# A hybrid attention decoder step on one core: the second sum of exponentials moves to PSUM and takes every second key tile, ScalarE casts the filler weights, and the masks of the row maxima go in pairs

## The chip, the cores and the metric

One core of a Trainium2 chip. The metric is the device time of one execution in microseconds (us), the median of several executions. PE is TensorE, PEld its weight loads, DVE is VectorE, ACT is ScalarE, POOL is GpSimd, SP the engine whose queue issues most DMAs.

## What is computed

One decoder layer: 2,048 prompt positions of width 1,024, and eight single decode positions with 512 cached positions each. The part that the change touches is the prompt's attention, eight heads of 64:

```python
s = einsum('bqhd,bkhd->bhqk', qb, kf) * SCALE
s = s + cb[:, :, :, None] - c[:, :, None, :]        # cumulated log forget gates
s = where(pos_k <= pos_q, s, -inf)
pr = softmax(s, axis=-1)
return einsum('bhqk,bkhd->bqhd', pr, vf)
```

Around it stand an input projection of 3,592 columns (q, k, v, forget gate, and the gates and operands of a chunked spatial mixing), silu gates, and an output projection of 1,024 by 1,024.

## The kernel before

The kernel has three stages. The first, up to about 590 us, makes the input projection in split precision: each fp32 operand is a rounded part (`hi`, the fp32r type) plus a remainder (`lo`), and three matmuls stand for one product. The second, 590 to 1181 us, is the prompt's attention with leftover projection work woven in. The third, from 1181 us, is the output projection.

**Attention, per head.** Two passes run over the scores. `maxima` (L897) takes each of the 16 query tiles (128 rows) in turn: it multiplies the tile with all keys at or before it, in pieces of at most 512 keys (`pieces`), each piece into one PSUM bank of the tag `tp`; on a tile's last piece a second small matmul adds the causal mask (weights `identb`, data `maskb`, both bf16, L917). A DVE minimum over the piece (L918, `mn`) frees the bank; signs are flipped, so a minimum is the row maximum. After four query tiles `shifts` (L926) turns the maxima and stores them as a row of the augmented queries.

`values` (L963) then takes one unit, 512 queries `c` of a head `h`, over its 4c+4 key tiles `kt`: two score matmuls into a bank of tag `sc` (with a mask on the diagonal tiles), one exponential on ACT into a ring tile `p` (L982), and, every eight tiles, a batch of `av` matmuls (`run_av`) that add `p` times the values into a bank of tag `av` (L1004). When a unit ends, ACT copies the upper half of `av` out (L1009, `at`) and DVE adds the lower half (L1010).

**The softmax denominators.** Beside that, the `p` tiles are summed for the denominators. POOL keeps the sum `acc` in SBUF (L989, L995) and takes most tiles. DVE keeps a second sum `accd` in SBUF: tiles 2 and 3 together (L991), then tiles 7 and 11 (L993), of units with c > 0. Two tiles into the diagonal (kt = 4c+1) POOL adds `accd` to `acc` (L997). Some 5 us of PE work later PE turns `acc` and DVE sums it (`add_up`, L1013 to L1019).

**Fillers.** Between these steps `fill` deals out matmuls of the projection that are left (tag `fl`) and, later, of the output projection. Their weights come 128 columns at a time (`fill_weights`, L772): POOL scales the raw rows by the norm's gain (L779, four instructions), POOL rounds them to `hi` (L781), POOL subtracts for `lo` (L782). The output projection's weights are rounded by ACT (`split`, L243) and subtracted by DVE (L248).

**Order.** PE's instructions run in the order in which the code emits them; the yields of `maxima`, `values` and the fillers interleave them, and `later` places follow-up work a set amount of PE work further on. The other engines run their own instructions in an order that a planner fixed beforehand by modelled times, each engine strictly one after another: an instruction that waits holds all behind it on its engine.

**PSUM.** The eight banks of stage 2 are dealt out in L1258: `sc` 2, `tp` 3 (also for all transposes), `av` 2, `fl` 1. In stage 3 the two halves of each output tile use `sc` and `av` (L1157). The 12 pieces of maxima that come before 590 us use a `tp` of two banks.

Of the kernel before, what the change touches and what calls it, by code (L numbers as in the profile page):

```python
# [9 lines left out]
F32 = mybir.dt.float32  # L10
# [4 lines left out]
ALU = mybir.AluOpType  # L15
AX = mybir.AxisListType
# [3 lines left out]
P = 128  # L20
# [5 lines left out]
HD = 64  # L26
# [23 lines left out]
FGAP = 1500.0  # L50
NSC = 2
NTP = 3
NAV = 2
UNITS = [(h, c) for h in range(6) for c in range(4)] + [(6, 0), (6, 1), (6, 2), (7, 0), (6, 3), (7, 1), (7, 2), (7, 3)]
AHEAD = 0.8
QLEAD = 6
# [22 lines left out]
def hymba_step(ctx, tc, x_prompt, x_sample, cache_k, cache_v, cache_logf, page_table, g_norm, w_in,  # L79
# [3 lines left out]
    nc = tc.nc  # L83
# [28 lines left out]
    def tname(t):  # L112
        cnt[0] += 1
        return f"{t}_{cnt[0]}"
# [10 lines left out]
    def s2(dt=F32, t="s2"):  # L125
        return wk.tile([P, 512], dt, tag="t2", name=tname(t))
# [6 lines left out]
    def bank(tag, n=512):  # L133
        pool, bufs = pool_of[tag]
        return pool.tile([P, n], F32, tag=tag, bufs=bufs, name=tname(tag))
# [37 lines left out]
    def mm(out, lhsT, rhs, start, stop, ns):  # L173
        Pe.last = nc.tensor.matmul(out, lhsT, rhs, start=start, stop=stop).ins  # L174
        pe(ns)
# [596 lines left out]
    def fill_weights(o, pair=None):  # L772
        hi, lo = (t.rearrange("p (k f) -> p k f", k=KT) for t in pair or (s4(F32R, "fh"), s4(F32R, "fl")))
        got = []

        def halves(half, raw):
            for k in range(4):
                kk = 4 * half + k
                nc.gpsimd.tensor_scalar(raw[:, k], raw[:, k], gT[:, kk:kk + 1], 0.0, op0=ALU.mult, op1=ALU.add)  # L779
            sl = slice(4 * half, 4 * half + 4)  # L780
            nc.gpsimd.tensor_scalar(hi[:, sl], raw, 1.0, 0.0, op0=ALU.mult, op1=ALU.add)  # L781
            nc.gpsimd.tensor_tensor(lo[:, sl], raw, hi[:, sl].bitcast(F32), op=ALU.subtract)  # L782
            got.extend((hi[:, k], lo[:, k]) for k in range(4 * half, 4 * half + 4))
        for half in range(2):
            raw = raw2().rearrange("p (k f) -> p k f", k=4)
            nc.sync.dma_start(raw, w[half * 512:(half + 1) * 512, o:o + P].rearrange("(k p) f -> p k f", p=P))
            later(FLAG * (1 + half), lambda half=half, raw=raw: halves(half, raw))
        return got
# [78 lines left out]
    def pieces(nk):  # L867

        n = (nk + 511) // 512
        if nk % n == 0 and (nk // n) % 2 == 0 and nk // n >= 256:  # L870
            return [(a * (nk // n), nk // n) for a in range(n)]
        return [(a * 512, min(512, nk - a * 512)) for a in range(n)]
# [24 lines left out]
    def maxima(hd):  # L897

        h = hd["h"]
        nxt = qhi.pop() if qhi else load_hi(h, 0)  # L900
        for c in range(2):
            q = nxt
            for i in range(8 * c, 8 * c + 8):
                if i == 2:
                    nxt = load_hi(h, 1)
                if i == 10 and h + 1 < NH:
                    qhi.append(load_hi(h + 1, 0))
                cut = pieces((i + 1) * P)
                if i % 4 == 0:
                    part = sm.tile([P, 4, len(cut)], F32, tag="mn", bufs=3, name=tname("mn"))  # L910
                for n, (c0, m) in enumerate(cut):
                    sp = bank("tp")[:, :m]
                    end = n == len(cut) - 1
                    mm(sp, q[:HD + 2, (i % 8) * P:(i % 8 + 1) * P], hd["k2"][:HD + 2, c0:c0 + m], True, not end,
                       max(m, 256) * 0.422)
                    if end:
                        mm(sp[:, m - P:], identb, maskb[:, 0], False, True, 56)  # L917
                    nc.vector.tensor_reduce(part[:, i % 4, n:n + 1], sp, axis=AX.X, op=ALU.min)  # L918
                    yield m * 0.422
                if i % 4 == 3:  # L920
                    shifts(h, i // 4, part)

    shifted = set()
# [39 lines left out]
    def values(at):  # L963
# [3 lines left out]
        for kt in range(4 * c + 4):  # L967
# [12 lines left out]
            p = ring[nt[0] % len(ring)]  # L980
            nt[0] += 1
            nc.scalar.activation(p[:, n0:], sp[:, n0:], AF.Exp, bias=zero1, scale=-1.0)  # L982
            if kt == 0 or kt == 2 and c:
                p0 = p
            elif kt == 1:
                if n0:
                    nc.gpsimd.memset(p[:, :n0], 0.0)
                    n0 = 0
                nc.gpsimd.tensor_tensor(acc, p0, p, op=ALU.add)  # L989
            elif kt == 3 and c:  # L990
                nc.vector.tensor_tensor(accd, p0, p, op=ALU.add)  # L991
            elif kt % 4 == 3 and kt < 4 * c:
                nc.vector.tensor_tensor(accd, accd, p, op=ALU.add)  # L993
            else:
                nc.gpsimd.tensor_tensor(acc[:, n0:], acc[:, n0:], p[:, n0:], op=ALU.add)  # L995
                if kt == 4 * c + 1:
                    nc.gpsimd.tensor_tensor(acc, acc, accd, op=ALU.add)  # L997

            def step(kt=kt, p=p, n0=n0, acc=acc, c=c, st=st, at=at):

# [110 lines left out]
    def out_products(i, hi, lo, xy, tags):  # L1111
        for f in range(2):
            fs = slice(f * 512, (f + 1) * 512)
            po = bank(tags[f])
            for n, k in enumerate(KORDER):
                wh, wl = wo_hl[k, f]
                mm(po, hi[:, k], wh, n == 0, False, 216)
                mm(po, hi[:, k], wl, False, False, 216)
                mm(po, lo[:, k], wh, False, n == KT - 1, 216)
                yield 648  # L1120
            nc.vector.tensor_tensor(xy[:, fs], xy[:, fs], po, op=ALU.add)
            yield 0
            if i == NT - 1:
                nc.scalar.dma_start(y[i * P:(i + 1) * P, fs], xy[:, fs])
        if i < NT - 1:
            nc.scalar.dma_start(y[i * P:(i + 1) * P], xy)
# [10 lines left out]
    def out_tiles():  # L1137

        gs = None
        for i in range(NT):  # L1140
            while i not in ins or not ins[i] or len(wo_hl) < 2 * KT:
                prepare(i)
                if last_phase[0]:
                    give()
                else:
                    yield -1
            for n in range(1, OAHEAD + 1):
                prepare(i + n)
            if i == 8:
                for _ in Pe.steps:  # L1150
                    pass
                while decoded[0] < B:
                    give()
                gs = decode_out()
            if gs is not None and i < 12:
                next(gs, None)
            yield from out_products(i, **ins.pop(i), tags=("sc", "av") if last_phase[0] else ("fl", "fl"))  # L1157

    mgen = all_maxima()
    mdone = [0.0]  # L1160
# [94 lines left out]

    seen = len(nc.cur_bb.bb.instructions)
    psb = ctx.enter_context(tc.tile_pool(name="psb", bufs=1, space=PSUM, reuse_waits="tile"))
    pool_of.update(sc=(psb, NSC), tp=(psb, NTP), av=(psb, NAV), fl=(psb, 1))  # L1258
    ring = []
    for t in [s8(t="p"), s8(t="p"), s4(t="p")]:  # L1260
        ring += [t[:, a:a + 512] for a in range(0, t.shape[1], 512)]
    accs = [s2(t="acc") for _ in range(2)]
    accd = s2(t="accd")
    Pe.side = 1e12
    while mdone[0] < AHEAD * MT:
        c = next(mgen)
# [66 lines left out]
```

## Time and profile before

| | |
|---|---|
| time, median of 3 runs | 1345.16 us (1342.2 to 1346.73) |
| profiled execution: its own time | 1347.51 us |
| profiled execution: span from first to last instruction | 1345.8 us |
| mean granted TensorE clock | 0.987 of 2.4 GHz |
| busy share of the span: PE, PEld, DVE, ACT, POOL | 97%, 75%, 53%, 32%, 43% |

A profile row of a group of instructions gives the line, the engine, the operation, output and input tiles with shapes, the count, then the busy time in us and the mean duration in ns, then the engine's idle time ahead of these instructions and what ended it. "issue" as the end of a wait means that the engine waited for nothing that the profile shows. Matmuls overlap, so the distance of their starts is the better measure of what one costs.

### The profile page before, as it was taken

The numbers are of one execution on the slowest core, as the hardware profiler recorded it, in microseconds if no ns is written. First come the engines' busy times: TensorE is split into PE (matmuls) and PEld (weight loads), VectorE is DVE, ScalarE is ACT, GpSimd is POOL, SyncE is SP. The second block draws the span as 40 slices with busy tenths as digits, with TensorE's granted clock in tenths as the row PEclk, the third lists the DMA queues.
The fourth block names the chain that finished last, engine by engine and source line by source line (L and its number), as shares of the span: only waits on it lengthen the run. The fifth ranks groups of instructions, "written<-read, shape, count | busy, mean of one in ns | idle before, by whom it ended". The sixth has DMA issues, their size and how long they took to land.

```text
span 1345.8 us, 19516 instructions
## 1 busy us (share of the span) xinstructions
PE 1304.6 (97%) x6544; PEld 1006.6 (75%) x6544; DVE 706.9 (53%) x1328; ACT 433.1 (32%) x781; POOL 574.6 (43%) x679
## 2 busy tenths in 40 slices
PE   6999999999999999999999999999999998999998
PEld 5999999999887877866666566666656664688877
DVE  4346654534678544266586555566565774322321
ACT  5542332222222111114453344434444456310100
POOL 3113343423223554416776666676757466400000
PEclk9999999999999999999998899999999998999999
DMA  6644353555113665634254854666375645463221
GB/s 217 188 119 112 87 142 116 155 140 158 52 48 99 187 184 148 159 97 127 78 138 85 181 138 126 177 182 169 95 192 135 172 119 196 135 238 117 107 77 49
DMA packets 170805, 183.09 MB, mean 136 GB/s; under 512 B 39402, under 2 KB 125866, under 8 KB 169138
## 3 DMA queue, kind: packets, MB, share of 16 engines
q1 hardware_dynamic: 166818, 173.08, 46.7%
q10 hardware_dynamic: 3488, 8.39, 1.6%
q8 instruction: 52, 0.85, 0.3%
q14 instruction: 47, 0.39, 0.1%
q0 software_dynamic: 400, 0.38, 0.1%
HBM read 121.53 MB, written 60.28 MB: 135 GB/s over the span
## 4 chain that ended last, share of the span: by engine, by line
PE 85%; DMA 6%; DVE 4%; ACT 2%; issue 1%; SPq 1%; POOL 1%; ACTq 0%; DVEq 0%; POOLq 0%
PE acc L174 36%; PE sc L174 15%; PE av L174 14%; PE fl L174 10%; PE tp L174 5%; PE tp L178 3%; PE pm L174 1%; DVE mn L918 1%; ACT p L982 1%; DMA xp<-in_x_prompt_dram 1%; DMA raw<-in_w_in_dram 1%; DMA q<-qk_hi 1%; DMA k<-qk_lo 1%; DMA q<-qk_lo 1%; DMA mrow<-mt 0%
## 5 line engine op out<-in xcount | busy, mean ns | idle before, releaser
L982 ACT ACTIVATE p<-sc,zero 128x512 f32<-128x512 f32 (+1 forms) x320 | 196.6, 623 | 173.9 <-PE sc L174 167.9
L995 POOL TENSOR_TENSOR acc<-acc,p 128x512 f32<-128x512 f32 (+3 forms) x184 | 194.1, 1055 | 125.2 <-ACT p L982 104.1
L918 DVE TENSOR_REDUCE mn<-tp 128x1 f32<-128x384 f32 (+6 forms) x320 | 186.9, 604 | 107.9 <-PE tp L174 105.6
L174 PE MATMUL acc<-wh,hh 128*128 128x384 f32 (+2 forms) x640 | 228.7, 357 | 0.0
L174 PE MATMUL acc<-wl,hh 128*128 128x384 f32 (+2 forms) x640 | 222.8, 348 | 1.0 <-DVE wl L256 0.9
L174 PE MATMUL acc<-wh,hl 128*128 128x384 f32 (+2 forms) x640 | 222.6, 348 | 0.6 <-DVE hl L248 0.6
L174 PE MATMUL sc<-q,k 128*128 128x512 f32 (+7 forms) x640 | 211.1, 407 | 10.6 <-ACT p L982 5.9
L174 PEld LDWEIGHTS sc<-q,k 128*128 128x128 f32 (+1 forms) x640 | 118.2, 197 | 35.3 <-ACT p L982 16.3
L174 PE MATMUL av<-p,vst 128*64 128x512 f32 (+3 forms) x640 | 135.4, 543 | 0.0
L174 PEld LDWEIGHTS acc<-wh,hh 128*128 128x128 f32 x640 | 120.7, 189 | 7.2 <-ACT hh L243 0.2
L174 PEld LDWEIGHTS acc<-wl,hh 128*128 128x128 f32 x640 | 120.9, 189 | 6.3 <-DVE wl L256 2.0
L174 PEld LDWEIGHTS acc<-wh,hl 128*128 128x128 f32 x640 | 120.3, 188 | 6.3 <-DVE hl L248 1.2
L174 PE MATMUL tp<-k,q 66*128 66x384 f32 (+6 forms) x320 | 120.3, 392 | 3.9 <-DVE mn L918 3.3
L236 POOL TENSOR_SCALAR sm<-sm 128x6 f32<-128x6 f32 (+3 forms) x84 | 20.3, 241 | 238.8 <-DVE sm L389 170.4
L174 PEld LDWEIGHTS av<-p,vst 128*64 128x64 f32 x640 | 47.9, 137 | 67.1 <-issue 57.6
L237 POOL TENSOR_TENSOR sm<-sm,mhalf 128x6 f32<-128x6 f32 (+3 forms) x84 | 89.6, 1067 | 6.7
L174 PE MATMUL sc<-wo,am 128*128 128x512 f32 x360 | 84.5, 390 | 0.0
L174 PE MATMUL av<-wo,am 128*128 128x512 f32 x360 | 84.2, 389 | 0.0
L174 PEld LDWEIGHTS tp<-k,q 66*128 66x128 f32 x320 | 61.2, 193 | 26.6 <-DVE mn L918 6.6
L174 PE MATMUL acc<-hh,wh 128*128 128x512 f32 x192 | 76.3, 397 | 4.9 <-DVE s L378 4.9
L174 PEld LDWEIGHTS av<-wo,am 128*128 128x128 f32 x360 | 67.5, 188 | 14.2
L174 PEld LDWEIGHTS sc<-wo,am 128*128 128x128 f32 x360 | 67.4, 188 | 14.1
(218 smaller groups left out, 2087.2 us busy)
## 6 DMA issues: line engine op xcount, KB each, us to landing
raw<-in_w_in_dram SPq DMA_DIRECT2D x40, 256.0 KB
kb<-in_cache_k_dram SPq DMA_DIRECT2D x32, 256.0 KB
k<-qk_hi SPq DMA_DIRECT2D x16, 512.0 KB
q<-qk_hi SPq DMA_DIRECT2D x64, 128.0 KB
vb<-in_cache_v_dram SPq DMA_DIRECT2D x32, 256.0 KB
g<-gm SPq DMA_DIRECT2D x16, 512.0 KB
xy<-in_x_prompt_dram SPq DMA_DIRECT2D x16, 512.0 KB
out_dram<-xy ACTq DMA_DIRECT2D x15, 512.0 KB
```

Source lines behind the costliest of these rows:

```text
L174: Pe.last = nc.tensor.matmul(out, lhsT, rhs, start=start, stop=stop).ins
L178: Pe.last = nc.tensor.transpose(out, in_, idn).ins
L236: nc.gpsimd.tensor_scalar(r, ss, inv_n, EPS, op0=ALU.mult, op1=ALU.add)
L237: nc.gpsimd.tensor_tensor(r, r, mhalf[:rows, :n], op=ALU.pow)
L918: nc.vector.tensor_reduce(part[:, i % 4, n:n + 1], sp, axis=AX.X, op=ALU.min)
L982: nc.scalar.activation(p[:, n0:], sp[:, n0:], AF.Exp, bias=zero1, scale=-1.0)
L995: nc.gpsimd.tensor_tensor(acc[:, n0:], acc[:, n0:], p[:, n0:], op=ALU.add)
```

## The change

- **Accumulator.** `accd` becomes a PSUM bank of a new tag `ad`; `av` goes from two banks to one. In units with c > 0, DVE copies tile 2 into `accd` and adds tiles 3, 5, 7, ... below 4c. POOL takes tiles 0 and 1, the even ones from 4 on, and the diagonal. The final sum of both moves from POOL to DVE. The SBUF buffer of `accd` goes back to the work pool. In stage 3 the second half of each output tile uses `ad`.
- **Filler weights.** The rounding to `hi` (L781) moves from POOL to ACT.
- **Maxima.** Query tiles go in pairs. The first tile's last piece is left open, its mask and minimum pending; the second tile begins with its own last piece; then come both masks, both minima, and the second tile's other pieces. `shifts` is called after the second pair of four tiles, as before after the fourth tile.

```diff
-NAV = 2
+NAV = 1
...
-            nc.gpsimd.tensor_scalar(hi[:, sl], raw, 1.0, 0.0, op0=ALU.mult, op1=ALU.add)
+            nc.scalar.copy(hi[:, sl], raw)
...
+                cuts = [pieces((j + 1) * P) for j in (i, i + 1)]
+                ends = []
+                for j, cut in zip((i, i + 1), (cuts[0], cuts[1][::-1])):
+                    for (c0, m) in cut:
+                        n = cuts[j - i].index((c0, m))
+                        end = n == len(cut) - 1
+                        sp = bank("tp")[:, :m]
+                        mm(sp, q[...], hd["k2"][:HD + 2, c0:c0 + m], True, not end, max(m, 256) * 0.422)
+                        if end:
+                            ends.append((sp, m, j, n))
+                            if j > i:
+                                for (sp, m_, _, _) in ends:
+                                    mm(sp[:, m_ - P:], identb, maskb[:, 0], False, True, 56)
+                                for (sp, _, j_, n_) in ends:
+                                    nc.vector.tensor_reduce(part[:, j_ % 4, n_:n_ + 1], sp, axis=AX.X, op=ALU.min)
+                        else:
+                            nc.vector.tensor_reduce(part[:, j % 4, n:n + 1], sp, axis=AX.X, op=ALU.min)
+                        yield m * 0.422
...
-            if kt == 0 or kt == 2 and c:
+            if kt == 0:
                 p0 = p
...
-            elif kt == 3 and c:
-                nc.vector.tensor_tensor(accd, p0, p, op=ALU.add)
-            elif kt % 4 == 3 and kt < 4 * c:
+            elif kt == 2 and c:
+                accd = bank("ad")
+                nc.vector.tensor_copy(accd, p)
+            elif kt % 2 == 1 and kt < 4 * c:
                 nc.vector.tensor_tensor(accd, accd, p, op=ALU.add)
             else:
                 nc.gpsimd.tensor_tensor(acc[:, n0:], acc[:, n0:], p[:, n0:], op=ALU.add)
                 if kt == 4 * c + 1:
-                    nc.gpsimd.tensor_tensor(acc, acc, accd, op=ALU.add)
+                    nc.vector.tensor_tensor(acc, acc, accd, op=ALU.add)
...
-            yield from out_products(i, **ins.pop(i), tags=("sc", "av") if last_phase[0] else ("fl", "fl"))
+            yield from out_products(i, **ins.pop(i), tags=("sc", "ad") if last_phase[0] else ("fl", "fl"))
...
-    pool_of.update(sc=(psb, NSC), tp=(psb, NTP), av=(psb, NAV), fl=(psb, 1))
+    pool_of.update(sc=(psb, NSC), tp=(psb, NTP), av=(psb, NAV), fl=(psb, 1), ad=(psb, 1))
...
-    accd = s2(t="accd")
```

## Rows read from the trace of the kernel before

**Rows 1.** The page: busy time of each engine, its share of the span and its instructions; and the granted TensorE clock in 40 slices of the span, in tenths.
```profile
PE 1304.6 (97%) x6544; PEld 1006.6 (75%) x6544; DVE 706.9 (53%) x1328; ACT 433.1 (32%) x781; POOL 574.6 (43%) x679
...
PEclk9999999999999999999998899999999998999999
```

**Rows 2.** Busy time by stretch: the stretch and its length, then busy us and instructions of PE, PEld, DVE, ACT and POOL, the granted clock, the DMA share and GB/s.
```profile
590.00:1100.00 510.00, 497.88 (x2458) 319.99 (x2459) 318.67 (x573) 221.74 (x402) 327.96 (x367) 0.98 0.55 141
1100.00:1181.00 81.00, 75.03 (x316) 45.14 (x315) 37.20 (x48) 38.29 (x66) 45.53 (x38) 0.92 0.53 167
1181.00:1345.80 164.80, 161.11 (x715) 130.38 (x713) 41.79 (x51) 12.82 (x14) 1.29 (x1) 1.00 0.33 118
```

**Rows 3.** The waits of PE between 590 and 1181 us: who waited for whom, us in total, times, the longest.
```profile
PE sc L174 <- ACT p L982: 5.9, 10, 1.5
PE sc L174 <- DMA q<-qk_hi: 3.9, 3, 2.5
PE tp L174 <- DVE mn L918: 3.3, 4, 2.3
PE fl L174 <- DVE sz L490: 1.3, 1, 1.3
```

**Rows 4.** Groups of instructions by form, the whole span: the masks of the maxima, and the weight loads of all masks (those of the maxima and those of the scores).
```profile
L174 PE MATMUL tp<-maskb,identb 128*128 128x128 bf16 x128 | 29.9, 233 | 0.0
...
L174 PEld LDWEIGHTS <-identb 128*128 128x128 bf16 x256 | 25.0, 98 | 39.2 <-issue 30.7
```

**Rows 5.** Timeline of PE about one masked piece (start us, duration us, what).
```profile
925.02 0.39 PE L174 MATMUL tp<-k,q 66*128 66x512 f32 x1
925.25 0.23 PE L174 MATMUL tp<-maskb,identb 128*128 128x128 bf16 x1
925.29 0.47 PE L174 MATMUL fl<-hh,fh 128*128 128x512 f32 x1
925.60 0.40 PE L174 MATMUL fl<-hl,fh 128*128 128x512 f32 x1
```

**Rows 6.** The chain of work that ended last, in order of time: one output half tile of stage 3 (start us, us, what).
```profile
1186.97 5.44 PE av L174 x24
```

**Rows 7.** Timeline of the weight loads about the masked piece of rows 5: the load for the mask.
```profile
925.24 0.10 PEld L174 LDWEIGHTS <-identb 128*128 128x128 bf16 x1 [0.27 <-issue]
```

**Rows 8.** The tile `accd`: its instructions with duration in ns (min/median/max), first and last start, form.
```profile
L991 DVE TENSOR_TENSOR accd<-p x24: 661/691/2058, 615.0 to 1144.0; 128x512 f32<-128x512 f32 x24
...
L993 DVE TENSOR_TENSOR accd<-accd,p x24: 675/1176/1737, 635.0 to 1159.8; 128x512 f32<-128x512 f32 x24
```

**Rows 9.** Groups of DVE by form between 590 and 1181 us: the two sums of `accd` in SBUF, the sum of `at` (SBUF) with `av` (PSUM).
```profile
L993 DVE TENSOR_TENSOR accd<-accd,p 128x512 f32<-128x512 f32 x24 | 27.6, 1148 | 11.8 <-ACT p L982 11.6
...
L1010 DVE TENSOR_TENSOR at<-at,av 64x512 f32<-64x512 f32 x32 | 21.6, 676 | 58.5 <-ACT at L1009 52.0 <-DMA vb<-in_cache_v_dram 3.6 <-DMA raw<-in_w_out_dram 3.0
...
L991 DVE TENSOR_TENSOR accd<-p 128x512 f32<-128x512 f32 x24 | 18.8, 785 | 8.0 <-ACT p L982 7.8
```

**Rows 10.** The tile `mxu`, where DVE multiplies one SBUF operand with one PSUM operand into SBUF (columns as in rows 8).
```profile
L507 DVE SCALAR_TENSOR_TENSOR mxu<-mxu,fl x8: 670/687/689, 642.0 to 1073.6; 128x512 f32<-128x512 f32 x8
```

**Rows 11.** Groups of POOL by form between 590 and 1181 us: sums of whole tiles, the final sum, the rounding of filler weights.
```profile
L995 POOL TENSOR_TENSOR acc<-acc,p 128x512 f32<-128x512 f32 x96 | 127.7, 1330 | 115.6 <-ACT p L982 101.3 <-ACT rt L1025 6.5 <-ACT mt L940 3.4
...
L997 POOL TENSOR_TENSOR acc<-acc,accd 128x512 f32<-128x512 f32 x24 | 31.7, 1320 | 1.4
...
L781 POOL TENSOR_SCALAR fh<-raw 128x512 fp32r<-128x512 f32 x22 | 14.1, 639 | 0.5
```

**Rows 12.** Timeline of ACT about the end of a unit with c = 3: four exponentials of the diagonal tiles in one row.
```profile
891.88 2.70 ACT L982 ACTIVATE p<-sc,zero 128x512 f32<-128x512 f32 x4 [0.82 <-PE sc L174]
```

**Rows 13.** Timeline of POOL in the same place: the sum of the second of these tiles (384 columns), and the final sum.
```profile
897.74 1.00 POOL L995 TENSOR_TENSOR acc<-acc,p 128x384 f32<-128x384 f32 x1
...
899.93 1.29 POOL L997 TENSOR_TENSOR acc<-acc,accd 128x512 f32<-128x512 f32 x1
```

**Rows 14.** Timeline of DVE: an instruction that waits for ACT with others queued behind it.
```profile
720.31 2.62 DVE L684 TENSOR_TENSOR_SCAN cc<-one,lfT 64x512 f32<-64x512 f32 x1 [1.70 <-ACT lfT L683]
```

**Rows 15.** Timeline of PE behind it.
```profile
723.57 0.50 PE L174 MATMUL tp<-k,q 66*128 66x512 f32 x1 [2.33 <-DVE mn L918]
```

**Rows 16.** Busy time by stretch, the stretches before and after that wait (columns as in rows 2).
```profile
717.00:724.20 7.20, 4.87 (x29) 3.70 (x27) 4.76 (x7) 3.23 (x5) 4.86 (x6) 1.00 0.19 53
724.20:731.02 6.82, 6.82 (x18) 4.66 (x17) 5.89 (x13) 3.08 (x7) 5.38 (x7) 0.50 0.26 80
```

**Rows 17.** Groups of ACT by form between 590 and 1181 us: roundings of output weights.
```profile
L243 ACT CAST wo<-raw 128x512 fp32r<-128x512 f32 x16 | 9.3, 616 | 4.5 <-DMA raw<-in_w_out_dram 4.5
```

**Rows 18.** Timeline of ACT: such a rounding that waited for its weights.
```profile
1075.10 0.62 ACT L243 CAST wo<-raw 128x512 fp32r<-128x512 f32 x1 [3.30 <-DMA raw<-in_w_out_dram]
```

**Rows 19.** Timeline of PE behind it.
```profile
1076.36 0.39 PE L174 MATMUL sc<-q,k 128*128 128x256 f32 x1 [1.52 <-ACT p L982]
```

**Rows 20.** Timeline of DVE at the border of two units: the last read of a unit's `av`.
```profile
751.69 0.67 DVE L1010 TENSOR_TENSOR at<-at,av 64x512 f32<-64x512 f32 x1
```

**Rows 21.** Timeline of PE at the same border: the first `av` matmul of the next unit.
```profile
753.17 1.08 PE L174 MATMUL av<-p,vst 128*64 128x512 f32 x4
```

More of the change, by code (lines that the diff above doesn't have):

```diff
@@ L902, in maxima @@
             q = nxt
-            for i in range(8 * c, 8 * c + 8):
+            for i in range(8 * c, 8 * c + 8, 2):
                 if i == 2:
@@ L907, in maxima @@
                     qhi.append(load_hi(h + 1, 0))
-                cut = pieces((i + 1) * P)
                 if i % 4 == 0:
[L910 to L920, printed above, removed]
+                    part = sm.tile([P, 4, i // 4 + 1], F32, tag="mn", bufs=3, name=tname("mn"))
+                cuts = [pieces((j + 1) * P) for j in (i, i + 1)]
[5 more added lines that the diff above has]
+                        sp = bank("tp")[:, :m]
+                        mm(sp, q[:HD + 2, (j % 8) * P:(j % 8 + 1) * P], hd["k2"][:HD + 2, c0:c0 + m], True, not end,
+                           max(m, 256) * 0.422)
+                        if end:
[8 more added lines that the diff above has]
+                        yield m * 0.422
+                if i % 4 == 2:
                     shifts(h, i // 4, part)
```

## The prediction

> **What bounds the kernel now.** I read the page first, then busy time by stretch, then PE's waits, then single places. The page gives PE 97% of the span and no other engine more than 53% [rows 1]; the reader is to see that only what changes PE's own stream or makes PE wait can move the time. By stretch, the change lies almost wholly in 590 to 1181 us: there DVE is busy 318.7 + 37.2 = 355.9 of 591 us (60%), POOL 373.5 (63%), ACT 260.0 (44%), PE 572.9 (97%), while after 1181 us PE is busy throughout and the clock is full; the granted clock is 0.98 and 0.92 in the two stretches of attention, so some microseconds ran at the lower of TensorE's two levels (1.2 of 2.4 GHz) [rows 2]. PE's waits there are short: 5.9 us for ACT's exponentials, 3.9 for a load of queries, 3.3 for the minima, 1.3 for a gate on DVE [rows 3]. So what can be won is: what PE spends on masks, about 10 us of waits, and the clock lost behind them.
>
> **Masks in pairs.** There are 128 masks in the maxima, and the 256 weight loads of all masks are preceded by 39.2 us of idle weight loading [rows 4]. One place shows the price of a single: from the piece to the second matmul after it PE takes 925.60 - 925.02 = 0.58 us. Two such matmuls of 512 columns alone would take 2 x 0.227 us, by the 5.44 us that 24 of them take in stage 3 [rows 5, 6]; the mask adds 0.13 us. Of that, 0.04 us is the mask's own distance to the next start, the rest comes after it (0.31 us for a matmul that otherwise takes 0.23): the next weights load beside a mask that is too short to cover it. Pairs make 64 groups of two. Nothing in the trace has two masks in a row. The second costs between 0.04 us (its stream alone) and 0.13 (as the first), so a pair saves 0 to 0.09 us, and all of them 0 to 5.8 us. I take 0.05 for the second, near the lower end, because no other weights of a different type have to be put back between the two: 64 x 0.08 = 5.1 us, all of it on PE's path.
>
> The row of the mask's weight load shows that it starts at 925.24, when the piece before has run out, and that nothing held it [rows 7]. The Trainium skill ("TensorE: Matmul & The Clock Gate", Step-by-step: what each phase is for) says that TensorE pulls a weight load ahead of the matmul in flight, which would leave nothing to save at the mask. The trace disagrees at this place. By that rule this term would be 0.
>
> **The sum in PSUM.** Removed from DVE: 24 x 785 ns + 24 x 1148 ns = 46.4 us. These sums are uneven, 661 to 2058 ns [rows 8, 9]. DVE's sum of `at` with a PSUM operand takes 676 ns, and the product of `mxu`, full 128 partitions with one operand in PSUM, 670 to 689 [rows 9, 10]. Per head the new units c = 1, 2, 3 have 1 + 3 + 5 sums, 3 copies and 3 final sums, so 72, 24 and 24 in all; at 0.68 us each (no row has DVE writing PSUM; 0.5 to 0.75 for the copies and sums is my bound) that is 81.6 us. DVE goes up by 35 us, from 60% to 66%. POOL loses 24 whole-tile sums, 24 final sums and 22 roundings: 31.9 + 31.7 + 14.1 = 77.7 us, from 63% to 50% [rows 11]. None of this is on PE's path by itself. PE pays only where DVE comes late: 3.3 + 1.3 us of waits now, and the clock behind them. More work on DVE speaks for more of that, the end of the 1.1 to 2 us sums, behind which minima queue, for less. Bounds: all of the 4.6 us gone, or as much again; I take -1.5 us, as the long instructions weigh more than the mean load at 66%. A `tp` bank is now held for one step more and two minima come at once, which eats one of about three steps of slack; I leave that in the bounds.
>
> **The final sum on DVE.** It must wait for POOL's sum of tile 4c+1, and all of DVE's queue waits with it: minima behind it, then PE's next `tp` bank; POOL in turn waits for DVE before the next diagonal tile. At one border the four diagonal exponentials end by 894.58, but POOL reaches the second of them at 897.74 and ends it at 898.74, more than 4 us late [rows 12, 13]. POOL will be less loaded, so such delays shrink. What a hold of DVE costs PE shows elsewhere: a scan waited 1.70 us for ACT, ran 2.62 us, and PE lost 2.33 us [rows 14, 15]; behind it the clock was 0.50 for 6.82 us [rows 16], half of which, 3.4 us, is PE work lost. Bounds: 0, and four such holds at 2.3 us, 9 us; I take +1 us, since most final sums come right after POOL's 1.3 us sum and three banks of scores to reduce lie between.
>
> **Roundings on ACT.** 22 at 616 ns (the same form for output weights [rows 17]) add 13.6 us to ACT, 44% to 46%. Each waits for POOL's four scalings, with exponentials queued behind it and PE behind those. The like has happened: a rounding waited 3.30 us for its data, and PE lost 1.52 us to the exponential behind it [rows 18, 19]. One in 16 such roundings did that; at that rate 22 cost 2.1 us. Bounds 0 to 5 us; I take +1.5, as POOL is less loaded.
>
> **One `av` bank.** The next unit's first `av` matmul must now wait until DVE has read the last one. At the tightest border DVE ended at 752.36 and that matmul started at 753.17, 0.81 us later [rows 20, 21]. So it costs nothing as things stand; if DVE comes later, some 0.5 us at each of the six borders from c = 3 to c = 0, 3 us at most. In stage 3 a half tile takes 5.44 us [rows 6] while DVE adds it in less than one, so one `ad` bank does there. I take 0 for both. The freed SBUF buffer has no price that a row shows.
>
> **Sum.** -5.1 - 1.5 + 1 + 1.5 = -4.1 us. The profiled execution's own time is 1347.51 us, its span 1345.8; it becomes 1343.4. The median of the runs shown, 1345.16, is 2.35 us below that execution, so the forecast of the median is 1341.
>
> **Rivals.**
> First, **DVE gates the attention** (slower). The final sums and the doubled count of sums that wait for exponentials hold DVE, minima come late, PE waits at `tp` and its clock falls. For it: DVE becomes the busiest engine after PE, strictly in order, and POOL's lateness of 4 us above; against it: PE loses only 3.3 us to minima now. It decides from where a hold exceeds about 2 us, as the one at 720 did. Price: six of the 24 final sums at 1 us, and two more stretches of 6.8 us at the lower clock at 3.4 us: 12.8 us; with the masks' gain 1345 - 5 + 13 = 1353. Chance 0.20.
> Second, **the second mask costs as much as the first** and the other terms cancel or cost their +2.5: then 1345 to 1347. This is also the case in which moving work between two engines off the path does nothing. For it: the masks' price is inferred from singles alone. Chance 0.24.
> Third, **relief beyond the sum** (much faster). With POOL at 50% and no long sums on DVE, the waits for DVE go and two of the stretches at the lower clock with them: -5.1 - 4.6 - 6.8 = -16.5, so 1329. For it: the stretch at 724 us hangs on a wait for DVE; against it: that wait came from a scan that stays, and other waits are for ACT and loads. Chance 0.16.
>
> **How the numbers follow.** My forecast, 1341 (1335 to 1346), has a chance of 0.40. About 0.3%, 4 us, is what a measurement of this kernel can tell from no change. Of the 0.40, 0.25 lies below 1341.1 by the bounds' pull, 0.15 above it. Faster: 0.25 + 0.16 + 0.05 of the second rival = 0.46. Same: 0.15 + 0.18 = 0.33, the second rival giving 0.18 and 0.01 to slower; slower: 0.20 + 0.01 = 0.21. The likeliest case has its own range of 1335 to 1346; for 8 in 10 it reaches up to most of the first rival and down to the third: 1329 to 1351.
>
> **What would show it.** Right: the second mask of a pair starts 0.05 us after the first and the next matmul is late once per pair; DVE's sums into `ad` take 0.68 us with no spread; POOL's busy time falls by about 78 us and DVE's rises by 35; PE's waits for minima stay under 5 us. Wrong: long waits of PE for `mn` or `p` just behind DVE's final sums or ACT's roundings of `fh`, DVE idle behind POOL in these sums, more stretches at clock 0.50, or a first `av` matmul of a unit that waits for `at`.

## The result, and the profile after

The changed kernel took 1353.08 us (median of 5 runs, 1351.39 to 1354.62) against 1346.73 us of the kernel before on the same chip: the ratio is 1.0049, 95% interval 1.0033 to 1.0064. It is slower, where 1341 was forecast. The profiled execution took 1352.08 us, its span is 1350.4.

The page's line of busy times (us, share of the span, instructions) and its row of PE's clock:

```profile
span 1350.4 us, 19504 instructions
...
PE 1303.1 (96%) x6544; PEld 1005.7 (74%) x6544; DVE 721.5 (53%) x1400; ACT 444.3 (33%) x805; POOL 490.3 (36%) x607
...
PEclk9999999999999999999999999999999998999999
```

PE does as many instructions as before, in less busy time, and its share has fallen: the time went into PE's gaps. Busy time by stretch (columns as in [rows 2]):

```profile
590.00:1100.00 510.00, 490.89 (x2438) 316.47 (x2438) 329.38 (x632) 230.06 (x422) 254.59 (x304) 0.99 0.53 140
1100.00:1181.00 81.00, 75.26 (x317) 43.39 (x316) 41.09 (x62) 40.29 (x70) 35.46 (x33) 0.92 0.53 162
```

Against [rows 2], PE is busy 7.0 us less in the first of the two stretches, POOL 73.4 us less, DVE only 10.7 us more. The clock is no worse (0.99 and 0.92 for 0.98 and 0.92). So neither a busier engine nor the clock accounts for the loss. PE's waits between 590 and 1181 us point to where it lies (who waited for whom, us in total, times, the longest):

```profile
PE tp L178 <- DVE mx L943: 5.1, 4, 1.8
PE sc L174 <- ACT p L991: 4.8, 10, 1.4
PE tp L174 <- DVE mn L925: 3.3, 6, 1.6
PE fl L174 <- DVE sz L490: 2.5, 2, 1.4
PE tp L174 <- ACT mt L949: 2.5, 5, 1.3
PE sc L174 <- DMA q<-qk_hi: 1.8, 2, 0.9
PE tp L174 <- DVE sm L1028: 1.6, 2, 0.9
PE tp L174 <- DVE mn L927: 0.6, 2, 0.3
PE tp L178 <- DVE sm L1029: 0.5, 2, 0.3
```

The exponentials and the loads of queries hold PE less than in [rows 3]. What has grown are the waits at `tp`: for `mx` 5.1 us (1.3 before), for the copy `mt` 2.5 (1.0), for the sums `sm` 2.1 in the two larger of their three rows (0.7). The same waits in the kernel before:

```profile
PE tp L178 <- DVE mx L934: 1.3, 1, 1.3
PE tp L174 <- ACT mt L940: 1.0, 2, 0.6
PE tp L178 <- DVE sm L1019: 0.7, 1, 0.7
```

The edited operations themselves behave as forecast (the tile `ad`: duration in ns, min/median/max, first and last start, forms):

```profile
L1003 DVE TENSOR_TENSOR ad<-ad,p x72: 666/692/700, 617.0 to 1164.3; 128x512 f32<-128x512 f32 x72
L1001 DVE COPY ad<-p x24: 666/684/695, 616.2 to 1148.2; 128x512 f32<-128x512 f32 x24
L1007 DVE TENSOR_TENSOR acc<-acc,ad x24: 669/686/689, 622.1 to 1168.3; 128x512 f32<-128x512 f32 x24
```

Where the sums of [rows 8] lay between 661 and 2058 ns, these lie between 666 and 700. One place shows how a late DVE reaches PE. First DVE from 1016 us (start, duration, idle before and what ended it), then POOL beside it, then PE:

```profile
1016.22 1.07 DVE L927 TENSOR_REDUCE mn<-tp 128x1 f32<-128x416 f32 x2
1017.21 0.15 DVE L939 TENSOR_REDUCE sm<-mn 128x4 f32<-128x12 f32 x1
1017.28 0.57 DVE L927 TENSOR_REDUCE mn<-tp 128x1 f32<-128x416 f32 x1
1017.78 0.68 DVE L1003 TENSOR_TENSOR ad<-ad,p 128x512 f32<-128x512 f32 x1
1018.38 1.23 DVE L942 TENSOR_SCALAR mx<-sm 128x4 fp32r<-128x4 f32 x1
1019.52 0.68 DVE L1003 TENSOR_TENSOR ad<-ad,p 128x512 f32<-128x512 f32 x1
1020.12 0.70 DVE L943 SCALAR_TENSOR_TENSOR mx<-sm,mx 128x4 fp32r<-128x4 f32 x1
```

```profile
1018.31 1.27 POOL L782 TENSOR_TENSOR fl<-raw,fh 128x512 fp32r<-128x512 f32 x1
1019.54 1.25 POOL L1005 TENSOR_TENSOR acc<-acc,p 128x512 f32<-128x512 f32 x1
```

```profile
1020.88 0.27 PE L178 MATMUL tp<-ident,mx 128*8 128x128 f32 x1 [1.67 <-DVE mx L943]
1021.50 0.47 PE L174 MATMUL tp<-k,q 66*128 66x448 f32 x1 [0.34 <-ACT mt L949]
1021.81 0.29 PE L174 MATMUL tp<-maskb,identb 128*128 128x128 bf16 x2
```

DVE works without a gap, yet the two tiny operations on `mx` (4 columns) take 1.23 and 0.70 us, where the median is 0.17: each ends just after POOL's instruction beside it (1019.61 after 1019.58, 1020.82 after 1020.79). PE's transpose of `mx` then waits 1.67 us, the next piece another 0.34 for its bank. Behind that the clock fell:

```profile
1022.40:1025.80 3.40, 3.40 (x9) 1.00 (x10) 2.09 (x4) 0.69 (x1) 0.00 (x0) 0.50 0.40 99
```

### The profile page after: what moved, and what is told of

Same layout as the page of the kernel before. It is cut to its first block, busy times and chain, and to the rows that moved or that the text cites. A ratio compares the mean times of both kernels' runs of the same rounds, so it can differ in the third digit from the quotient of the medians.

```text
span 1350.4 us, 19504 instructions
## 1 busy us (share of the span) xinstructions
PE 1303.1 (96%) x6544; PEld 1005.7 (74%) x6544; DVE 721.5 (53%) x1400; ACT 444.3 (33%) x805; POOL 490.3 (36%) x607
## 4 chain that ended last, share of the span: by engine, by line
PE 82%; DVE 6%; DMA 5%; issue 2%; ACT 2%; SPq 2%; POOL 1%; ACTq 0%; DVEq 0%; POOLq 0%
PE acc L174 35%; PE sc L174 15%; PE fl L174 9%; PE av L174 8%; PE ad L174 6%; PE tp L174 5%; PE tp L178 3%; DMA q<-qk_hi 1%; PE pm L174 1%; DVE mn L927 1%; DVE mn L925 1%; DMA xp<-in_x_prompt_dram 1%; DMA k<-qk_hi 1%; DVE wl L256 1%; ACT p L991 1%
## 5 line engine op out<-in xcount | busy, mean ns | idle before, releaser
L1005 POOL TENSOR_TENSOR acc<-acc,p 128x512 f32<-128x512 f32 (+3 forms) x160 | 158.8, 993 | 177.3 <-ACT p L991 135.3
L174 PE MATMUL sc<-q,k 128*128 128x512 f32 (+7 forms) x640 | 205.1, 398 | 7.1 <-ACT p L991 4.8
L927 DVE TENSOR_REDUCE mn<-tp 128x1 f32<-128x320 f32 (+5 forms) x192 | 118.1, 629 | 57.9 <-PE tp L174 56.5
L925 DVE TENSOR_REDUCE mn<-tp 128x1 f32<-128x512 f32 (+7 forms) x128 | 66.8, 562 | 48.7 <-PE tp L174 48.4
L174 PE MATMUL ad<-wo,am 128*128 128x512 f32 x360 | 84.2, 389 | 0.0
L174 PEld LDWEIGHTS ad<-wo,am 128*128 128x128 f32 x360 | 67.5, 188 | 14.2
```

The source lines that it names most:

```text
L925: nc.vector.tensor_reduce(part[:, j_ % 4, n_:n_ + 1], sp, axis=AX.X, op=ALU.min)
L927: nc.vector.tensor_reduce(part[:, j % 4, n:n + 1], sp, axis=AX.X, op=ALU.min)
```

## The experiments

My first theory was the first rival's: DVE's new sums make it late, and PE pays. Its rival: the pairs do, since a `tp` bank is held one step longer and two minima become ready at once. All runs of one batch share a chip and runs of the kernel before, whose median was 1344.3, 1346.73, 1346.12, 1346.88 and 1346.88 us in the five batches. Intervals are of 95%. A ratio is not the quotient of two medians; where the two differ most, in h3, the ratio is 1.0015 and the quotient 1.0027.

**One part at a time.**

e1: the masks' hunk of the diff alone.

```
-            for i in range(8 * c, 8 * c + 8):
+            for i in range(8 * c, 8 * c + 8, 2):
...
```

> The pairs of masks alone, all else as before. Theory (the accumulator loads DVE, which comes late to the turn of the maxima and to the minima): faster than before by 3 to 6 us, about the 4.3 us by which PE's excess around the masks of the maxima fell in the changed kernel; PE's waits for DVE (minima, turned maxima, gates) stay near the 6.6 us of before. Rival A (two minima at once and a held bank make DVE late): within 2 us of before or slower, with 3 us or more of new waits of PE for minima or for the turned maxima, as in the changed kernel. Rival B (any edit reshuffles the planned order, and the sum of small waits is luck): anywhere from -8 to +6 us, with waits in other places than in the changed kernel.

Measured: 1349.48 us, 1.0036 (1.0014 to 1.0058). The longest of its waits at `tp`, 590 to 1181 us:

```profile
PE tp L174 <- ACT mt L949: 3.1, 5, 1.6
PE tp L178 <- DVE sm L1028: 2.7, 2, 2.4
PE tp L178 <- DVE mx L943: 2.2, 2, 1.8
```

e2: the accumulator's hunk, and one bank each for `av` and `ad`.

```
+            elif kt == 2 and c:
+                accd = bank("ad")
+                nc.vector.tensor_copy(accd, p)
...
```

> The accumulator in PSUM alone: one av bank, every second tile and the final sum on DVE, casts and masks as before. Theory: slower than before by 7 to 12 us (the changed kernel's +6, plus what the pairs save), with PE's waits for DVE at 10 us or more and DVE idle behind POOL some 15 us in the final sums. Rival A: within 3 us of before. Rival B: no relation to the other runs.

Measured: 1344.07 us, 0.9998 (0.9979 to 1.0016). The sum in PSUM costs nothing that the interval shows: my theory, 7 to 12 us, fell.

e3: the roundings alone; e4: roundings and pairs.

```
-            nc.gpsimd.tensor_scalar(hi[:, sl], raw, 1.0, 0.0, op0=ALU.mult, op1=ALU.add)
+            nc.scalar.copy(hi[:, sl], raw)
```

> The filler weights rounded by ACT alone. Theory: within 2 us of before; ACT idle behind POOL's scalings by 15 to 30 us, of which PE feels under 2 us in waits for exponentials. Rival C (ACT behind POOL is what costs): slower by 4 us or more, with PE's waits for exponentials up from 5.9 us to 9 or more.

> Pairs and casts without the accumulator: the changed kernel with the old sums. Theory: faster than before by 2 to 6 us, so 8 to 12 us faster than the changed kernel. Rival A: no faster than before. Rival B: not the sum of the pairs' and the casts' runs, off by 4 us or more.

Measured: e3 1346.67 us, 1.0019 (1.0003 to 1.0034); e4 1350.11 us, 1.0041 (1.0023 to 1.0059). The loss comes with the pairs.

**What in the pairs costs.**

f1: as e1, with no step of the attention between the two last pieces, so the first bank is held for less time.

```
+                        if end and j == i:
+                            held = m * 0.422
+                            continue
```

> Pairs alone, but nothing is emitted between the open last piece of the first tile and the last piece of the second, so the first bank is held for one matmul and not for a step of other work. Theory now (the bank that stays held, out of three, makes the other users of these banks, transposes of the sums and of the maxima, wait): most of the pairs' loss of 5 us goes, 1340 to 1346. Rival (two minima at once make DVE late, however short the hold): no better than the pairs, 1347 to 1352, since two scores in a row now bring their minima even closer.

Measured: 1355.43 us, 1.0062 (1.0040 to 1.0085), worse than theory and rival had it. PE's waits at `tp`, 590 to 1181 us:

```profile
PE tp L178 <- DVE mx L945: 6.2, 2, 5.5
...
PE tp L174 <- DVE mn L927: 4.2, 5, 1.5
PE tp L178 <- DVE sm L1031: 2.9, 2, 2.3
...
PE tp L178 <- DVE sm L942: 1.6, 1, 1.6
```

The wait of 5.5 us is a single place. There a DVE sum of two SBUF tiles lasted 5.53 us, while POOL ran five instructions without a gap, and PE stood still:

```profile
683.29 5.53 DVE L1003 TENSOR_TENSOR accd<-p 128x512 f32<-128x512 f32 x1
691.54 0.37 PE L178 MATMUL tp<-ident,sm 128*4 128x128 f32 x1 [5.54 <-DVE mx L945]
```

In the profiled execution this place alone is about the size of what f1 takes longer than e1 (spans of 1352.6 and 1348.1 us). From the start of the last piece of a pair's first tile to the end of its minimum, a `tp` bank is held 1.35 us in f1 and 2.42 in e1 (medians); the two minima start 0.48 us apart in both.

f2: the pairs' order with each mask right behind its piece, and the first minimum emitted only with the second, to hold the bank without saving a mask.

```
+                            mm(sp[:, m - P:], identb, maskb[:, 0], False, True, 56)
                             ends.append((sp, m, j, n))
```

> Pairs in the order of the change, with each mask issued at once behind its own piece as before, and only the first tile's minimum held back until the second's: a bank is held as long, two minima come at once, and no mask is saved. Theory and its rival alike: slower than the pairs alone by the 4 to 5 us that the masks save, 1352 to 1356. If it is no slower than the pairs, the saving on masks is not worth what the trace shows around them.

Measured: 1348.99 us, 1.0025 (1.0009 to 1.0041), where theory and rival both said 1352 to 1356. But the run does not test the hold: the planner put the first minimum right behind its own mask all the same. One pair of f2, PE and DVE:

```profile
847.34 0.23 PE L174 MATMUL tp<-maskb,identb 128*128 128x128 bf16 x1
847.61 0.49 DVE L924 TENSOR_REDUCE mn<-tp 128x1 f32<-128x320 f32 x1 [0.21 <-PE tp L174]
848.53 0.34 PE L174 MATMUL tp<-k,q 66*128 66x384 f32 x1
```

The minimum starts 0.92 us before the second tile's last piece, and the bank is held 1.15 us (median). On PE, DVE, ACT and POOL the trace of f2 has the same instructions in the same order as that of g2 below; f2 is a second measurement of g2.

f3: the pairs with four `tp` banks and one of `av`; f4: the kernel before with the same banks.

```
-NTP = 3
-NAV = 2
+NTP = 4
+NAV = 1
```

> Pairs alone, with one bank for av and four for the pieces. Theory (held bank): the waits of PE at these banks for ACT and DVE fall from 12 us to under 6, the masks' saving shows, 1337 to 1343, at least 3 us below the next run. Rival (minima late on DVE): 1345 or more, as the DVE queue is the same.

> The control of the last: the kernel before with one bank for av and four for the pieces. Theory: 1340 to 1345, somewhat better than before as PE's waits for minima go; one av bank costs nothing. Rival: as before, 1344 to 1347; if one av bank costs, PE's waits for av's readers appear.

Measured: f3 1346.87 us, 1.0010 (0.9992 to 1.0028); f4 1346.26 us, 1.0008 (0.9985 to 1.0032). With a fourth bank the pairs cost nothing that these intervals show; it doesn't make them a gain either, which my theory expected (1337 to 1343).

**How much is only a shifted order, and do later transposes help.**

g1: one unrelated due time moved. g2: the pairs' order of pieces, with single masks and each minimum at once. g3: the pairs, with the small transposes of `mx` and of the reciprocal sums due later. g4: the kernel before with these due times.

```
g1:    -ACLAG = 5000.0
       +ACLAG = 5200.0
g2:    +for j, cut in zip((i, i + 1), (cuts[0], cuts[1][::-1])):
       +    for (c0, m) in cut:          (then mask and minimum as before)
g3,g4: -SLAG = 3000.0                    -later(2000, done)
       +SLAG = 4500.0                    +later(3500, done)
```

> The kernel before with one due time that has nothing to do with the change moved a little (the transposes of a unit's sums 5200 ns instead of 5000 after its end). It adds and removes no instruction, only shifts which of them stand next to each other. Theory 'the pairs cost something of their own (minima bunched, a tp bank held)': within 0.15% of before, 1344 to 1349 us. Theory 'differences of 0.3 to 0.4% are what any reshuffling of the order gives, and no cause of its own stands behind them': more than 0.25% away from before, to either side.

> The order of pieces of the pairs (the second tile's pieces backwards) with single masks, and every minimum right behind its own piece: no bank held, no two minima at once. If the hold and the bunching cost the time: within 0.15% of before, 1344 to 1349 us, and PE's waits for tp in 590 to 1190 us stay at about 6 us. If the order itself costs it (the last minima of four tiles come nearer to the scaling of mx): 0.25% or more above before, 1350 us.

> Pairs alone, and the two small transposes that wait for DVE (of mx and of the reciprocal sums) come due 1500 ns later. If the loss is PE waiting for a late mx and late sums behind two minima: most of the 5 us is back, 1343 to 1347 us, with waits for mx and sm under 3 us. If the loss is the held bank and the short delays at each pair: no change from the pairs alone, 1349 to 1352 us.

> The kernel before with the same two due times 1500 ns later; the control of the pairs with later transposes. PE waits only 1.3 us for mx and 0.7 for sums before, so both theories expect no change beyond 0.15%: 1343 to 1349 us. If it moves as much as the pairs with later transposes, those show nothing on the pairs.

Measured: g1 1345.54 us, 0.9991 (0.9975 to 1.0006); g2 1349.72 us, 1.0029 (1.0013 to 1.0045); g3 1351.71 us, 1.0041 (1.0021 to 1.0061); g4 1342.53 us, 0.9971 (0.9951 to 0.9992). The order alone costs something, which I had not put on my list; later transposes don't repair the pairs, but they help the kernel before, which neither theory expected.

**Is it the order itself.**

h1: g2 with four `tp` banks and one of `av`. h2: the kernel before with every tile's pieces backwards, so that the end pieces stay as far apart as before. h3: g2 with g1's due time. h4: e2 with g4's due times.

```
h2: -for n, (c0, m) in enumerate(cut):
    +for n, (c0, m) in list(enumerate(cut))[::-1]:
```

> The pairs' order of pieces with single masks, four tp banks and one av bank. If the order costs because three banks are too few for it: as the kernel before with four tp banks, 1344 to 1348 us (ratio 0.999 to 1.002). If the order costs by itself, wherever the banks are: 0.25% or more above that, 1349 to 1351 us; then the masks' saving is what brought the pairs with four banks back to no change.

> The kernel before with the pieces of every tile backwards, masks single: the end pieces are as far apart as before, but each tile begins with its end. If the neighbourhood of two end pieces costs: no change, within 0.15% of before. If leaving the forward order costs (or the tile's last piece, which the maximum of four tiles waits for, must not be a long one): 0.2% or more slower.

> The pairs' order with single masks and the due time of the null edit (5200 ns instead of 5000). If the order has a cost of its own: 0.2 to 0.4% above before again, as without the null edit. If its 0.29% was a reshuffling: anywhere within 0.3% of before, more likely under 0.15%.

> The sum of exponentials in PSUM without pairs and without casts on ACT, and the two small transposes due 1500 ns later. If the later transposes have a gain of their own: 0.2 to 0.35% faster than before, 1341 to 1344 us, as the kernel before with them. If their gain was a reshuffling: within 0.15% of before, as the sum in PSUM alone.

Measured: h1 1357.04 us, 1.0070 (1.0037 to 1.0103); h2 1346.51 us, 0.9990 (0.9967 to 1.0013); h3 1350.54 us, 1.0015 (0.9991 to 1.0038); h4 1341.52 us, 0.9949 (0.9919 to 0.9978), the best version found. In h1 one place stands out. DVE, POOL and PE there (start, duration):

```profile
726.02 5.04 DVE L691 TENSOR_TENSOR sm<-sm,cc 64x1 f32<-64x1 f32 x1
```

```profile
726.76 0.62 POOL L781 TENSOR_SCALAR fh<-raw 128x512 fp32r<-128x512 f32 x1
727.35 1.26 POOL L997 TENSOR_TENSOR acc<-acc,p 128x512 f32<-128x512 f32 x1
728.57 1.26 POOL L782 TENSOR_TENSOR fl<-raw,fh 128x512 fp32r<-128x512 f32 x1
729.78 1.27 POOL L997 TENSOR_TENSOR acc<-acc,p 128x512 f32<-128x512 f32 x1
```

```profile
732.31 0.79 PE L174 MATMUL fl<-hh,fh 128*128 128x512 f32 x1 [5.27 <-DVE sz L490]
```

A DVE operation on one column lasted 5.04 us, while POOL ran these four without a gap and ended at 731.05; DVE's ended at 731.06, and PE lost 5.27 us. In the kernel before the same operation took 0.14 us. Part of h1's cost is thus an accident of where the order puts things, as in f1, and not evidence against the bank.

**The pairs in two other surroundings.**

i1: the changed kernel without its pairs (e2 and e3 together). i2: h4 with the masks' hunk of the diff. Both are made of hunks shown above.

> The changed kernel without its pairs: sum in PSUM and casts on ACT, masks as before. If the pairs alone make the changed kernel slower: the sum of the two parts measured alone, -0.02 + 0.19, so 0.0 to 0.2% above before (1346 to 1349 us), and at least 0.25% under the changed kernel's 1.0049. If the three parts hurt each other (DVE busier and minima bunched): near before, under 0.05%, and nearly all of the 0.49% appears only with the pairs; if sum and casts hurt each other: 0.35% or more above before.

> The best version so far (sum in PSUM, later transposes; 0.51% under before) with the masks in pairs. If the pairs cost wherever three banks serve the scores, by the 0.36% measured alone to the 0.70% measured with later transposes: 0.15% below before to 0.2% above. If the pairs' cost was one of the surrounding: 0.4% or more below before, as without them or better by the 5 us that the masks save.

Measured: i1 1344.36 us, 0.9984 (0.9967 to 1.0002); i2 1349.12 us, 1.0016 (0.9995 to 1.0037). This settles which part is at fault: the masks' hunk, and not the other two. With three `tp` banks, the same hunk costs 0.36% (e1 against before), 0.65% (after against i1: 1.0049/0.9984), 0.70% (g3 against g4) and 0.67% (i2 against h4); with four, 0.02% (f3 against f4). The interval of e1 lies wholly above 1, and in the other three pairs of runs with three banks the two intervals do not overlap; those of f3 and f4 reach some 0.2% to either side. Beside the other two parts the hunk costs 0.65% and alone 0.36%, but the intervals don't tell these two apart.

## Why the prediction was wrong, point by point

For the accounting I took all of PE's records from 590 to 1190 us, and from each distance between two starts the time of the stream itself: 13 ns and its columns at 2.4 GHz, which makes the 227 ns of [rows 6] for 512 columns, 0.422 ns a column for `av`, 108 ns for a small transpose and nothing for masks. What is left is put by its place, in us; a wait is a gap of over 150 ns, a short delay is less, and the clock's column is the work lost in stretches at the lower level. It is one profiled execution of each kernel; only differences between rows mean anything, and of the clock's column not much. As g2 and f2 are the same program, their rows show the scatter, some 2 us in the waits and in the sum:

```
kernel                      clock  masks of maxima  short, into tp  waits, into tp  all else   sum
before                       14.7        19.5            1.9             5.4          59.1    100.6
g2 order alone               16.7        19.0            2.0             5.5          59.1    102.3
f2 the same as g2            16.7        18.5            2.1             7.4          59.8    104.5
e1 pairs                     13.0        14.9            6.0            10.7          58.4    103.0
f1 pairs, minima adjacent     9.0        13.3            5.9            19.1          60.2    107.5
f4 four tp banks              7.8        18.3            0.3             6.2          63.2     95.8
f3 pairs, four tp banks      11.9        12.6            1.6            11.9          61.1     99.1
i1 change without pairs       9.6        18.9            2.9             6.2          60.8     98.4
after                        10.1        15.5            6.2            12.5          59.7    104.0
```

**Masks in pairs, -5.1 us: right at the masks, wrong as time.** The second mask of a pair is cheap, as forecast: from the end piece's start to the second matmul after it, less the streams, a single costs 0.142 us (median) and a pair 0.20 in e1 and some 0.21 in after. The second mask starts 0.07 us after the first (median). A pair of after on PE:

```profile
849.86 0.40 PE L174 MATMUL tp<-k,q 66*128 66x512 f32 x1
850.10 0.29 PE L174 MATMUL tp<-maskb,identb 128*128 128x128 bf16 x2
850.20 0.75 PE L174 MATMUL sc<-q,k 128*128 128x512 f32 x2
```

The accounting shows the gain, -4.6 us in e1 and -4.0 in after, each against before. The step that failed is the phrase "all of it on PE's path", and behind it the sentence on the `tp` bank held for one step more, where I wrote "I leave that in the bounds" and gave it no price. It has one: in e1 the places where PE takes a `tp` bank lose 4.1 us more in short delays and 5.3 us more in waits, together twice what the masks give; against g2, which has the same order without pairs, 4.0 and 5.2, for 4.1 gained at the masks; in after against i1, 3.3 and 6.3 us. What the pairs change there is two things at once: the first bank is held 2.42 us for 1.15 in g2, and the two minima start 0.48 us apart for 1.20 (medians). f1 holds the first bank 1.35 us and keeps the minima as close: the short delays stay (5.9), and of its 19.1 us of waits 5.5 are the one long DVE sum. So a shorter hold of the first bank did not help, which speaks for the two minima; but no run holds a bank without bringing the minima together, so no experiment parts the two. I read it thus, which is argued and not shown: three banks had no step of slack to give away, since `mx`, the sums and the scores share them and wait for one DVE queue. f3's fourth bank fits that: it takes the short delays away (1.6 against 6.0) but not the waits (11.9), which are mostly for DVE, behind whatever bank. In time the fourth bank brings the pairs to within 0.02% of the same banks without them.

**The order, which I priced at nothing without saying so.** The hunk also turns the second tile's pieces round. g2, f2 and h3 put that alone at 0.29, 0.25 and 0.15% (h3's interval includes no change), h1 at 0.62% over f4 with the accident of 5 us in it, while g1, a shift with no change of content, and h2, all tiles backwards, stay within 0.1%. The span times the granted clock of each timed execution, which leaves out the time lost to the clock, rises by 2.5, 2.2 and 2.6 us in g2, f2 and h3, and by 4.6 in e1 (means over 12 executions each, 11 in g2, whose twelfth shows a clock of 0.938 that doesn't fit its time; standard errors 0.5 to 0.8). So the order costs some 2.5 us, about half of e1's loss, and pairing on top of it costs some 2 us net (standard error about 1). That it is the neighbourhood of two end pieces (1.39 us apart in g2, 3.31 before) is argued from h2; through what it costs, the accounting does not show (g2's extra 1.7 us stand in the clock's column), and it stays open.

**The sum in PSUM, -1.5 us: not contradicted.** 36.2 us of sums were added on DVE (66.2 + 16.4 - 46.4) and the long ones are gone; the bare effect was 0.9998 (0.9979 to 1.0016), which can't tell -1.5 us from nothing, and 0.9984 with the roundings. DVE's busy time rose by 14.6 us and not 35. One reason that I missed gives 8 us of the difference: with POOL relieved, DVE's products into `ga` fell from 1158 to 803 ns and those into `wo` from 987 to 807. POOL's busy time fell by 83 us (78 forecast).

**The final sum, +1 us: its hold is real, its price is not seen.** DVE's waits in after, 590 to 1181 us:

```profile
DVE acc L1007 <- POOL acc L1005: 18.8, 15, 3.0
DVE ad L1003 <- ACT p L991: 16.5, 22, 3.3
```

15 of 24 final sums waited, 18.8 us in all, up to 3.0 us, beyond the 2 us from which the first rival was to decide. PE didn't pay in e2 and i1, where the maxima don't go in pairs; that the pairs are the reason is likely and not tested by itself. That rival gave 1353 and the time is 1353, but its mechanism is not the one at work: i1 has 13 of its holds, 16.7 us in all, and is not slower. That the number came out is luck.

**Roundings on ACT, +1.5 us: not settled, the sign neither.** 22 casts at 615 ns, 616 forecast; they waited 24.3 us for POOL's scalings. e3 gives +0.19% or 2.5 us, i1 against e2 -0.14%, within the intervals. **One `av` bank, 0:** right; no wait of PE for it stands among the waits above.

**The range** ended at 1351, since neither the price of the bunching nor that of the order was in it; the chance of "slower" hung on the one rival and not on the part that I had counted as the gain.

## What to carry to other kernels

A saving on the bounding engine that is bought by holding a buffer longer and making two results ready at once must be charged with the waits of everyone who shares that buffer and that queue; count the buffers and the users first, for here a gain of 4 to 5 us was paid for with 9 to 10. Test the order alone as well as the edit: turning pieces round cost 0.15 to 0.29% here. Look in the trace, too, whether an experiment did what its source says: f2's held minimum was not held. And where a waiting step hangs on a strict queue, a later due time is cheap to try: it gave 0.29% on the kernel before, 0.49% on the sum in PSUM (h4 against e2), and nothing with the pairs. The best version found is the sum in PSUM with later transposes, 1341.52 us.

## What the runs showed of the hardware

DVE operations of some kinds are held while POOL works on SBUF: sums and products of two SBUF operands, and the scaling of `mx`. The operations on `mx` in after (ns, min/median/max):

```profile
L942 DVE TENSOR_SCALAR mx<-sm x24: 131/166/1233, 590.1 to 1112.3; 128x4 fp32r<-128x4 f32 x24
L943 DVE SCALAR_TENSOR_TENSOR mx<-sm,mx x24: 132/164/1206, 591.2 to 1113.0; 128x4 fp32r<-128x4 f32 x24
```

Of the 62 operations on `mx`, 19 took over 250 ns, and every one of these ended within 0.04 us after the end of a POOL instruction; so did all 16 in e1 and all 20 in the kernel before. On `mx` the holds cost DVE 11 to 13 us in these three kernels and 16.9 in f1. None of the 120 sums and copies with `ad` was held, none of the minima from PSUM (the 109 of 512 columns took 615 to 693 ns), and none of the 32 reciprocals of `sm` (157 to 179 ns) though they lie in SBUF. The sums of [rows 8] follow the same rule: all 21 that took over 0.8 us ended 0.54 to 0.55 us after the end of a POOL instruction. Between 590 and 1190 us no DVE instruction with a PSUM operand took over 0.70 us in any kernel here, while sums into `accd` in SBUF took up to 5.53 us (f1; 4.61 in g3, 3.92 in f3, 3.76 in f2). Such long holds come and go with the timing: f2 and g2 are the same program, and g2's trace has no sum over 2.1 us. The Trainium skill ("Advanced Engine Details and Errata", GPSIMD Details) says that GpSimd shares a read and a write interface with VectorE and conflicts with instructions of two SBUF inputs or in a 2-port mode. The rows agree (which mode an instruction ran in they do not show), and they show the length of the hold: until POOL's running instruction ends, or with a chain of them the whole chain, as the 5.04 us of h1 and the 5.53 of f1. It explains the spread of [rows 8], which I had only noted. It doesn't explain why the wait for `mx` grew: `mx` was held as often before (20 times) as after (19), so what changed is when these steps come and not how long they take.

The clock spreads the executions of one program: in eleven of g4's twelve the mean granted clock went from 0.989 to 0.996 while the span went from 1344.9 to 1334.2 us (the twelfth shows 0.944 at 1342.8 us, which does not fit). g4's gain lies there: its span times its clock did not fall (+0.6 us, standard error 0.5), while its clock is 0.992 on average against 0.989 of the kernel before in the same batch. What in the order gives it more of the clock is not shown.
